# Two-layer transformer step on one core: weight rounding, probability scaling and the differential heads' small operations change engine or shape

## The chip, the cores and the metric

The kernel runs on one core of one Trainium2 chip, in one launch. The metric is device microseconds. Three runs of the kernel before took 935.11, 935.13 and 935.72 us, a median of 935.13 us.

## The reference

256 tokens of width 1024 (one batch) go through two transformer blocks, all in fp32. What matters here is the second block: 16 meta tokens are put in front (272 keys), one input projection feeds two attentions, and a gated sum of the two goes through an output projection and a gated MLP.

The first of the second block's attentions is banded: 16 query heads on 4 key heads, head width 64, a window of 128 positions, all meta keys, and a sink logit that has no value; its softmax therefore runs over 272 scores and the sink. The second is differential: 8 heads with two query/key pairs each,

```python
p = jax.nn.softmax(s, axis=-1)
a = p[:, :, 0] - lam * p[:, :, 1]
o = rms_norm(einsum(a, v), subln_gain) * (1.0 - lambda_init)
```

dense over the 272 keys. The first block has a smaller banded attention (8 query heads on 2 key heads, 256 keys and a sink) beside a retention layer.

## The kernel before

**Split products.** fp32 accuracy comes from three products per matrix: the weight and the activation are each written as a rounded high part and the low remainder, and high*high, high*low and low*high are added in PSUM (`PASS`). So each weight must be split on chip. Weights come as 272 units of 128x1024 (`wstream`). `fetch` (L283 to L302) does one unit: SP issues the load into `raw` (4 buffers); `hi` is `raw` rounded; `lo` is `raw - hi`, on DVE in two pieces of 512 columns (L301). The rounding has two forms. Where `hi_pool` is false, ACT does it in two pieces of 512 columns (L299). Where it is true, GpSimd (POOL) does all 1024 columns in one instruction (L296). `next_unit` splits one unit ahead of the one that is asked for. `hi_pool` is true for two units at the very start and, set after the V projections of the second block, for the 38 units that are split during its two attentions; it is set false again when the branch projections begin.

**Second block's attentions.** `keys` and `proj_a` project two feature tiles (48 matmuls of 128x128 by 256 or 272 columns); `rope_T` copies the result out on ACT (L501, L503), swaps halves with four small DMAs that ACT issues (L505, L506), and multiplies and adds on DVE (L507) and POOL (L508, L511). `stack_q` and `stack_k` split the result again: `qe`, `qo`, `ks` are rounded on ACT, their low parts come from POOL (L521, L522, L537) and DVE (L536). The scores follow on TensorE (L544, L545, mask L547).

**Banded attention** (`sink_attention`, `sink_softmax`): per query head a row minimum on DVE (`mn`, L552), the exponential on ACT with its row sum (`p`, L562), a reciprocal on DVE (`rc`, L564), and the scaling of the 272 (first block: 128 or 256) probabilities to `pn` on ACT (L565). Then four heads are transposed on TensorE (L580), split into `pt` on ACT and DVE (L327, L328), and multiplied with V (`o_ps`, L584). There are 32 such heads and query tiles in the second block, 16 in the first.

**Differential heads** (L929 to L989): for each of 8 heads and each of 2 query tiles, two scores, two `mn`, two exponentials into `p` (L942, 6 buffers) with their sums in two 1-wide tiles `den0`, `den1`; then on DVE, per query tile, `e2` (L946), `rc` (L949), `rl` (L951), all one element per row, and `a` = `p0` + `rl` * `p1` (L954). After both query tiles `a` is transposed (L960, L965), copied by ACT (L962, L967), multiplied with V (`od_ps`, L972 to L974), normalized and transposed again.

**Order.** The tile framework sets each engine's instruction order when the program is built: a planner runs the whole program through its own model of costs and gives each engine a fixed list. The engines then run these lists in order, with semaphores between them. So matmuls of later projections stand between those of the attention, where the planner expected room. PSUM banks and SBUF tiles are shared by tag as `BANKS`, `ROT` and `BUFS` say.

Of the kernel before, what the change touches and what calls it, by code (L numbers as in the profile page):

```python
# [12 lines left out]
AF = mybir.ActivationFunctionType  # L13
ALU = mybir.AluOpType
# [7 lines left out]
NKEY = NTOK + NMETA  # L22
EPS = 1e-6
# [4 lines left out]
# products of parts (weight, x), 0 high, 1 low; what needs the low part of x goes last where x comes late  # L28
PASS = ((0, 0), (0, 1), (1, 0))
PARTS = (((0, 0), (1, 0)), ((0, 1),))  # L30
WB = 5  # units of split weights on chip
AHEAD = 1  # units split before they are asked for
LAG = 4  # last units of an output projection, done token tile by token tile
# [4 lines left out]
VB1 = 2  # the second half of V of the differential heads follows this head group of the window attention  # L38
PIECE = 512  # columns of a unit split at a time
# PSUM banks by tag, and which of them each kind of use takes in turn, part by part of the program  # L40
# [8 lines left out]
# tiles per name in each phase  # L49
# [10 lines left out]
# ---------------------------------------------------------------- host layout  # L60
# [162 lines left out]
# ---------------------------------------------------------------- the kernel  # L223
class Body:
# [22 lines left out]
    # ---- small helpers  # L247
    def banks(self, name):
        """how the spare PSUM bank "x" is shared out from here on"""
        self.rot = {k: [0, v.split()] for k, v in ROT[name].items()}  # L250
# [25 lines left out]
    def t(self, shape, name, dt=F32, tag=None):  # L276
        """a tile of the current phase"""
        tag = tag or name
        return self.rp.tile(shape, dt, tag=tag, bufs=self.bufs.get(tag, 1), name=name)
# [24 lines left out]
    def spare(self, skip, tags):  # L304
        """big tiles that nothing else needs for now hold units, from the skip-th that is still to be fetched"""
        u = self.un + skip
        for tag in tags:
            if tag == "DE":
                self.place[u] = [self.bp.tile([P, UC], F32R, tag="D", name=f"hi{u}"),
                                 self.bp.tile([P, UC], F32R, tag="E", name=f"lo{u}")]  # L310
                u += 1
            else:
                t = self.bp.tile([P, 2, 2, UC], F32R, tag=tag, name=f"w{u}")
                for i in range(2):
                    self.place[u] = [t[:, i, 0], t[:, i, 1]]
                    u += 1
# [84 lines left out]
    def sumsq(self, h, np_=P):  # L401
        """sum of squares of h [np_, 1024] (or of two psum halves) per partition, in two halves"""
        nc = self.nc
        xn = self.t([P, D], "xn")
        ss = self.sm(2, "ss")
        for c in range(2):
            s = slice(512 * c, 512 * c + 512)
            src = h[c] if isinstance(h, list) else h[:np_, s]
            nc.scalar.activation(out=xn[:np_, s], in_=src, func=AF.Square, accum_out=ss[:np_, c:c + 1])
        return xn, ss  # L410
# [16 lines left out]
    def to_T(self, xn, c, dst, t0, np_=P):  # L427
        """four feature tiles of xn (half c) transposed, split into dst"""
        nc = self.nc
        b = self.tp([P, 4, np_], "xt_ps")  # L430
        for j in range(4):
            k = 4 * c + j
            nc.tensor.transpose(b[:, j, :], xn[:np_, k * P:(k + 1) * P], self.ident[:np_, :np_])
        self.split(dst[:, 0, 4 * c:4 * c + 4, t0:t0 + np_], dst[:, 1, 4 * c:4 * c + 4, t0:t0 + np_], b)
# [11 lines left out]
    def mm_a(self, out, unit, XT, n0, n1, kn=8, j=0):  # L446
        """out[128, n1-n0] = W^T X^T for the j-th 128 columns of the unit"""
        nc = self.nc
        wv = [w.rearrange("p (k c) -> p k c", k=kn) for w in unit]
        i = 0  # L450
        last = 3 * kn - 1
        for k in range(kn):
            for a, b in PASS:
                nc.tensor.matmul(out, wv[a][:, k, j * P:(j + 1) * P], XT[:, b, k, n0:n1],  # L454
                                 start=(i == 0), stop=(i == last))
                i += 1

    def mm_b(self, out, unit, XT, t0, t1, kn, k0, c0, cn, start, stop):
        """out[tokens, cn] += X[tokens, k-tiles] W"""
        nc = self.nc  # L460
        wv = [w.rearrange("p (k c) -> p k c", k=kn) for w in unit]
        i = 0
        last = 3 * kn - 1
        for k in range(kn):
            for a, b in PASS:
                nc.tensor.matmul(out, XT[:, b, k0 + k, t0:t1], wv[a][:, k, c0:c0 + cn],  # L466
                                 start=(start and i == 0), stop=(stop and i == last))
                i += 1

    def mm_group(self, out, us, XT, t0, t1, kn, cn):  # L470
        """out[tokens, cn] = X[tokens] W over all units; the low parts of X come last, they are ready last"""
        nc = self.nc
        ws = [[w.rearrange("p (k c) -> p k c", k=kn) for w in u] for u in us]
        seq = [(j, k, a, b) for part in PARTS for j in range(len(us)) for k in range(kn) for a, b in part]
        for i, (j, k, a, b) in enumerate(seq):
            nc.tensor.matmul(out, XT[:, b, kn * j + k, t0:t1], ws[j][a][:, k, :cn],  # L476
                             start=(i == 0), stop=(i == len(seq) - 1))

    def group_b(self, XT, toks, kn, nh, cn, name):
        """X @ W for one group of columns over nh units; one psum bank per token range"""  # L480
# [6 lines left out]
    def rope_T(self, ps, m, n, tab, half, out=None, scale=1.0):  # L487
        """ps [128, m, n] feature-major, times scale; returns fp32 SBUF tile"""
        nc = self.nc
# [19 lines left out]
        if out is None:  # L509
            out = t1  # L510
# [3 lines left out]
    def stack_q(self, qf):  # L514
        """qf [128, 2, 256] -> QE, QO [128, 2, 256]: hi and lo stacked on the contraction rows"""
        nc = self.nc
# [8 lines left out]
    def stack_k(self, kf, n):  # L525
        """kf [128, n] (two heads) -> [(KS, KL)] * 2"""
# [14 lines left out]
    def scores(self, out, q, k, k0, k1, mask=None):  # L541
        """out[128, k1-k0] = q^T k (all four partial products), mask = (index, first column)"""
# [12 lines left out]
    def sink_softmax(self, s, n, nsink, out):  # L555
        """s [128, n + 1] in PSUM, negated scores, the last column for the sink; out [128, n] = softmax(-s)"""
# [8 lines left out]
        nc.scalar.activation(out=out, in_=p[:, :n], func=AF.Copy, scale=rc)  # L565

    def sink_attention(self, q, kst, vs, sink, ktiles, masks, OT, c, qt):
        """one kv head and one query tile: four q heads"""
# [43 lines left out]
    def out_proj(self):  # L612
        """psum banks [t][c] of a product X @ W of 1024 columns"""
# [11 lines left out]
    def out_last(self, acc, jobs, t, major=False):  # L625
        """the last units for token tile t, one bank after the other"""
# [6 lines left out]
    # ---- block 1  # L633
    def block1(self):
# [22 lines left out]
        # v of the retention, token-major  # L657
# [53 lines left out]
        # sliding window attention  # L711
# [20 lines left out]
        # gates and branches  # L732
# [38 lines left out]
        for t in range(2):  # L771
# [8 lines left out]
            # relu(r z)^2 = r^2 relu(z)^2: the row factor of the norm goes on after the second product  # L780
# [44 lines left out]
    # ---- block 2  # L825
    def block2(self):
# [6 lines left out]
        for t in range(2):  # L833
            self.out_last(acc, jobs, t)
            # both norms in one: with m = mean(h^2) + eps and hf = h * g_fin, x2 = hf / sqrt(m) and its own mean
            # square plus eps is (mean(hf^2) + eps * m) / m
# [44 lines left out]
        def v_T(m, name):  # L881
            """V^T of m feature tiles, transposed: per token range a psum bank [tokens, m * 128]"""
# [19 lines left out]
        self.hi_pool = True  # L902
# [24 lines left out]
        for pr in range(4):  # L927
            kb = keys()
            q = self.stack_q(self.rope_T(self.proj_a(XT, name="q_ps"), 2, NTOK, rope_b, 32, scale=-0.125))  # L929
            for m in range(2):  # L930
                h = 2 * pr + m
                am = []
                e2 = self.sm(2, "e2")
                for qt in range(2):
                    ps, den = [], []
                    for e in range(2):
# [4 lines left out]
                        d = self.sm(1, f"den{e}")  # L941
                        nc.scalar.activation(out=p[:, :NKEY], in_=s, func=AF.Exp, bias=nm, scale=-1.0, accum_out=d)  # L942
                        ps.append(p)
                        den.append(d)
                    # den0 * (softmax 0 - lam softmax 1): the norm that follows takes den0 out, its eps times den0^2
                    nc.vector.scalar_tensor_tensor(out=e2[:, qt:qt + 1], in0=den[0], scalar=EPS, in1=den[0],  # L946
                                                   op0=ALU.mult, op1=ALU.mult)
                    rc = self.sm(1, "rc")
                    nc.vector.reciprocal(rc, den[1])  # L949
                    rl = self.sm(1, "rl")  # L950
                    nc.vector.scalar_tensor_tensor(out=rl, in0=rc, scalar=self.nlam, in1=den[0],  # L951
                                                   op0=ALU.mult, op1=ALU.mult)
                    a = self.t([P, NKEY + 2], "a")
                    nc.vector.scalar_tensor_tensor(out=a[:, :NKEY], in0=ps[1][:, :NKEY], scalar=rl,  # L954
                                                   in1=ps[0][:, :NKEY], op0=ALU.mult, op1=ALU.add)
# [65 lines left out]
        def post(t, acc, gain):  # L1021
            """x[t] += rmsnorm(acc[t]) * gain, by halves"""
# [73 lines left out]
# ---------------------------------------------------------------- launch  # L1096
# [34 lines left out]
```

## Time and profile before

| | |
|---|---|
| median of three runs | 935.13 us |
| span of the profiled execution, first to last instruction | 927.7 us |
| TensorE (PE) busy | 895.6 us, 97% |
| DVE busy | 632.9 us, 68% |
| ACT busy | 495.1 us, 53% |
| POOL busy | 221.8 us, 24% |
| granted TensorE clock, mean | 0.994 |

The profile gives the span of the profiled execution, and no device time of its own beside it; the median lies 7.4 us above the span. Busy shares are means over stages. The second block's attentions run from about 433 to 632 us of the span. PE's busy time is that of pipelined matmuls whose ends are modelled: a matmul of 256 columns is shown with some 285 ns, while 48 of them take 5.74 us, one each 120 ns. A hole of less than about 160 ns between two matmuls is therefore not seen as idle time.

### The profile page before, as it was taken

The numbers are of one execution on the slowest core, as the hardware profiler recorded it, in microseconds if no ns is written. First come the engines' busy times: TensorE is split into PE (matmuls) and PEld (weight loads), VectorE is DVE, ScalarE is ACT, GpSimd is POOL, SyncE is SP. The second block draws the span as 40 slices with busy tenths as digits, with TensorE's granted clock in tenths as the row PEclk, the third lists the DMA queues.
The fourth block names the chain that finished last, engine by engine and source line by source line (L and its number), as shares of the span: only waits on it lengthen the run. The fifth ranks groups of instructions, "written<-read, shape, count | busy, mean of one in ns | idle before, by whom it ended". The sixth has DMA issues, their size and how long they took to land.

```text
span 927.7 us, 16499 instructions
## 1 busy us (share of the span) xinstructions
PE 895.6 (97%) x6188; PEld 819.8 (88%) x6188; DVE 632.9 (68%) x1177; ACT 495.1 (53%) x1100; POOL 221.8 (24%) x219
## 2 busy tenths in 40 slices
PE   6999899999999999999979999999999999999997
PEld 4899889998889999978978888798999799999996
DVE  5556887577755455565889999997567665655554
ACT  4544368555554554554237786576455454444442
POOL 3012550011000000012795757652011100000000
PEclk9999999999999999999999999999999999999999
DMA  8675554468666656663744344343466666665551
GB/s 287 242 212 154 160 154 137 137 204 290 206 189 183 185 185 191 189 203 111 211 135 144 99 126 123 105 135 104 135 186 211 232 197 195 187 190 186 183 160 45
DMA packets 48128, 160.20 MB, mean 173 GB/s; under 512 B 6432, under 2 KB 8224, under 8 KB 48048
## 3 DMA queue, kind: packets, MB, share of 16 engines
q1 hardware_dynamic: 43376, 153.95, 52.7%
q10 hardware_dynamic: 4672, 5.20, 2.0%
q8 instruction: 48, 0.79, 0.4%
q14 instruction: 32, 0.26, 0.1%
HBM read 151.83 MB, written 2.10 MB: 166 GB/s over the span
## 4 chain that ended last, share of the span: by engine, by line
PE 77%; DVE 8%; DMA 5%; POOL 4%; issue 3%; ACT 2%; ACTq 0%; SPq 0%; POOLq 0%; DVEq 0%
PE op L466 21%; PE fi_ps L454 12%; PE f_ps L454 9%; PE gate_ps L454 7%; DVE lo L301 5%; PE ru_ps L454 3%; PE gr_ps L454 2%; PE bd_ps L454 2%; PE vr_ps L476 2%; PE bs_ps L454 2%; DMA sw<-t 2%; DMA raw<-in_wstream_dram 2%; PE vb_ps L476 2%; PE fi_ps L476 1%; PE au_ps L454 1%
## 5 line engine op out<-in xcount | busy, mean ns | idle before, releaser
L301 DVE TENSOR_TENSOR lo<-raw,hi 128x512 fp32r<-128x512 f32 x536 | 385.9, 762 | 196.7 <-ACT hi L299 188.3
L299 ACT CAST hi<-raw 128x512 fp32r<-128x512 f32 x456 | 258.8, 618 | 240.0 <-issue 84.4
L466 PE MATMUL op<-hi,hid 128*128 128x512 f32 x416 | 131.3, 396 | 0.0
L454 PE MATMUL fi_ps<-xf2t,hi 128*128 128x256 f32 x640 | 115.8, 283 | 0.0
L454 PEld LDWEIGHTS fi_ps<-xf2t,hi 128*128 128x128 f32 x640 | 100.3, 191 | 1.0
L466 PEld LDWEIGHTS op<-hi,hid 128*128 128x128 f32 x416 | 76.3, 188 | 16.7
L454 PE MATMUL fi_ps<-xf2t,lo 128*128 128x256 f32 x320 | 90.5, 283 | 0.0
L466 PE MATMUL op<-lo,hid 128*128 128x512 f32 x208 | 81.4, 393 | 0.0
L454 PE MATMUL f_ps<-xf1t,hi 128*128 128x256 f32 x448 | 81.4, 283 | 0.0
L454 PEld LDWEIGHTS f_ps<-xf1t,hi 128*128 128x128 f32 x448 | 70.7, 191 | 1.3
L454 PE MATMUL f_ps<-xf1t,lo 128*128 128x256 f32 x224 | 63.3, 282 | 0.0
L454 PEld LDWEIGHTS fi_ps<-xf2t,lo 128*128 128x128 f32 x320 | 61.2, 191 | 0.0
L296 POOL TENSOR_SCALAR hi<-raw 128x1024 fp32r<-128x1024 f32 x40 | 48.8, 1223 | 35.8 <-PE k_ps L454 13.5
L415 POOL TENSOR_SCALAR e<-ss 128x1 f32<-128x1 f32 (+1 forms) x11 | 3.3, 303 | 223.8 <-ACT py L1027 195.0
L795 POOL TENSOR_TENSOR sq<-relu 128x512 f32<-128x512 f32 x14 | 15.8, 1129 | 152.4 <-ACT relu L792 152.4
L454 PE MATMUL q_ps<-x2t,hi 128*128 128x256 f32 x256 | 49.6, 287 | 0.0
L454 PE MATMUL gate_ps<-x1t,hi 128*128 128x256 f32 x256 | 49.4, 287 | 0.0
L454 PE MATMUL gate_ps<-x2t,hi 128*128 128x256 f32 x256 | 48.7, 284 | 0.0
L466 PEld LDWEIGHTS op<-lo,hid 128*128 128x128 f32 x208 | 39.0, 188 | 9.2
L454 PEld LDWEIGHTS f_ps<-xf1t,lo 128*128 128x128 f32 x224 | 42.8, 191 | 0.1
L454 PEld LDWEIGHTS gate_ps<-x2t,hi 128*128 128x128 f32 x256 | 40.0, 189 | 1.1 <-issue 1.0
L454 PEld LDWEIGHTS q_ps<-x2t,hi 128*128 128x128 f32 x256 | 40.2, 189 | 0.7 <-issue 0.5
(297 smaller groups left out, 2090.3 us busy)
## 6 DMA issues: line engine op xcount, KB each, us to landing
raw<-in_wstream_dram SPq DMA_DIRECT2D x272, 512.0 KB, 3.7
sw<-t ACTq DMA_DIRECT2D x40, 64.0 KB, 3.4
x<-in_x_dram SPq DMA_DIRECT2D x3, 512.0 KB, 6.8
sw<-t ACTq DMA_DIRECT2D x40, 34.0 KB, 2.5
sw<-t ACTq DMA_DIRECT2D x8, 128.0 KB, 4.7
g_pre<-in_gains_dram SPq DMA_DIRECT2D x2, 512.0 KB, 6.2
x<-hf SPq DMA_DIRECT2D x2, 512.0 KB, 2.7
x<-x SPq DMA_DIRECT2D x2, 512.0 KB, 5.8
```

The costliest lines, as they stand in the source:

```text
L296: nc.gpsimd.tensor_scalar(out=hi, in0=raw, scalar1=1.0, scalar2=0.0, op0=ALU.mult, op1=ALU.add)
L299: nc.scalar.copy(hi[:, c:c + PIECE], raw[:, c:c + PIECE])
L301: nc.vector.tensor_sub(lo[:, c:c + PIECE], raw[:, c:c + PIECE], hi[:, c:c + PIECE].bitcast(F32))
L415: nc.gpsimd.tensor_scalar(out=e[:np_], in0=ss[:np_, 0:1], scalar1=1.0 / D, scalar2=EPS, op0=ALU.mult, op1=ALU.add)
L454: nc.tensor.matmul(out, wv[a][:, k, j * P:(j + 1) * P], XT[:, b, k, n0:n1], start=(i == 0), stop=(i == last))
L466: nc.tensor.matmul(out, XT[:, b, k0 + k, t0:t1], wv[a][:, k, c0:c0 + cn], start=(start and i == 0), stop=(stop and i == last))
L476: nc.tensor.matmul(out, XT[:, b, kn * j + k, t0:t1], ws[j][a][:, k, :cn], start=(i == 0), stop=(i == len(seq) - 1))
L795: nc.gpsimd.tensor_tensor(out=q, in0=r, in1=r, op=ALU.mult)
```

## The change

Three edits; comments were removed as well, which changes no instruction.

- `hi_pool` is no longer set true ahead of the second block's attentions, so their 38 units are rounded on ACT in two pieces (L299) in place of POOL in one (L296).
- The scaling of the banded probabilities (`pn`) goes from an ACT activation to a DVE `tensor_scalar`, in both blocks, since both use `sink_softmax`.
- In the differential heads all four exponentials of a head come first, their sums in two 2-wide tiles; `rc`, `rl` and `e2` are done once for both query tiles, two elements per row; then the two `a`.

```diff
@@ sink_softmax
-        nc.scalar.activation(out=out, in_=p[:, :n], func=AF.Copy, scale=rc)
+        nc.vector.tensor_scalar(out=out, in0=p[:, :n], scalar1=rc, scalar2=None, op0=ALU.mult)
@@ block2
         kts = [(0, P), (P, P), (NTOK, NMETA)]
-        self.hi_pool = True
@@ block2, differential heads
-                am = []
-                e2 = self.sm(2, "e2")
+                den = [self.sm(2, f"den{e}") for e in range(2)]
+                ps = []
                 for qt in range(2):
-                    ps, den = [], []
                     for e in range(2):
                         ...
-                        d = self.sm(1, f"den{e}")
-                        nc.scalar.activation(out=p[:, :NKEY], in_=s, func=AF.Exp, bias=nm, scale=-1.0, accum_out=d)
+                        nc.scalar.activation(out=p[:, :NKEY], in_=s, func=AF.Exp, bias=nm, scale=-1.0,
+                                             accum_out=den[e][:, qt:qt + 1])
                         ps.append(p)
-                        den.append(d)
-                    nc.vector.scalar_tensor_tensor(out=e2[:, qt:qt + 1], in0=den[0], scalar=EPS, in1=den[0],
-                                                   op0=ALU.mult, op1=ALU.mult)
-                    rc = self.sm(1, "rc")
-                    nc.vector.reciprocal(rc, den[1])
-                    rl = self.sm(1, "rl")
-                    nc.vector.scalar_tensor_tensor(out=rl, in0=rc, scalar=self.nlam, in1=den[0],
-                                                   op0=ALU.mult, op1=ALU.mult)
+                rc = self.sm(2, "rc")
+                nc.vector.reciprocal(rc, den[1])
+                rl = self.sm(2, "rl")
+                nc.vector.scalar_tensor_tensor(out=rl, in0=rc, scalar=self.nlam, in1=den[0],
+                                               op0=ALU.mult, op1=ALU.mult)
+                e2 = self.sm(2, "e2")
+                nc.vector.scalar_tensor_tensor(out=e2, in0=den[0], scalar=EPS, in1=den[0],
+                                               op0=ALU.mult, op1=ALU.mult)
+                am = []
+                for qt in range(2):
                     a = self.t([P, NKEY + 2], "a")
-                    nc.vector.scalar_tensor_tensor(out=a[:, :NKEY], in0=ps[1][:, :NKEY], scalar=rl,
-                                                   in1=ps[0][:, :NKEY], op0=ALU.mult, op1=ALU.add)
+                    nc.vector.scalar_tensor_tensor(out=a[:, :NKEY], in0=ps[2 * qt + 1][:, :NKEY],
+                                                   scalar=rl[:, qt:qt + 1], in1=ps[2 * qt][:, :NKEY],
+                                                   op0=ALU.mult, op1=ALU.add)
                     am.append(a)
```

## Rows read from the trace of the kernel before

**Rows 1.** Windows: us, then busy us (instructions) by engine, PEclk, DMA share, GB/s.

```profile
460.00:490.00 30.00, 24.95 (x187) 23.70 (x186) 24.95 (x39) 11.08 (x29) 27.81 (x20) 0.94 0.47 139
490.00:540.00 50.00, 47.74 (x349) 41.79 (x348) 47.56 (x113) 37.57 (x99) 32.00 (x27) 1.00 0.44 126
...
632.00:660.00 28.00, 27.95 (x214) 25.95 (x215) 20.58 (x58) 16.55 (x55) 2.14 (x4) 1.00 0.39 113
460.00:620.00 160.00, 148.77 (x1098) 134.23 (x1097) 146.87 (x306) 101.71 (x275) 110.69 (x93) 0.99 0.42 123
```

**Rows 2.** Waits of PE over the span: total us, times, longest us.

```profile
PE s L544 <- POOL qe L521: 4.2, 1, 4.2
PE o_ps L584 <- DVE pt L328: 3.7, 2, 2.0
...
PE s L544 <- ACT p L562: 2.1, 1, 2.1
```

**Rows 3.** Timeline of POOL, 455 to 486 us: start us, us, engine, line.

```profile
465.33 1.49 POOL L296 TENSOR_SCALAR hi<-raw 128x1024 fp32r<-128x1024 f32 x1
...
468.47 1.71 POOL L508 TENSOR_TENSOR sw<-sw,rope_b 128x512 f32<-128x512 f32 x1
470.15 1.48 POOL L296 TENSOR_SCALAR hi<-raw 128x1024 fp32r<-128x1024 f32 x1
471.72 1.76 POOL L521 TENSOR_TENSOR qe<-t,qe 64x512 fp32r<-64x512 f32 x1
```

**Rows 4.** Timeline of ACT, same stretch; idle time before and its releaser in brackets.

```profile
460.55 0.60 ACTq L506 DMA_DIRECT2D sw<-t  x1
...
468.54 0.62 ACT L519 CAST qe<-t 64x512 fp32r<-64x512 f32 x1 [4.17 <-POOL t L511]
```

**Rows 5.** Timeline of PE, same stretch.

```profile
473.53 0.59 PE L544 MATMUL s<-ks,qe 128*128 128x272 f32 x1 [4.25 <-POOL qe L521]
```

**Rows 6.** Groups by form, 430 to 660 us: busy us, mean ns | idle before.

```profile
L301 DVE TENSOR_TENSOR lo<-raw,hi 128x512 fp32r<-128x512 f32 x100 | 88.7, 927 | 9.7 <-POOL hi L296 5.0 <-ACT hi L299 4.6
...
L296 POOL TENSOR_SCALAR hi<-raw 128x1024 fp32r<-128x1024 f32 x38 | 46.7, 1232 | 34.9 <-PE k_ps L454 13.5 <-PE vb_ps L476 11.8 <-PE gate_ps L454 3.2
...
L565 ACT ACTIVATE pn<-p,rc 128x272 f32<-128x272 f32 x32 | 15.9, 520 | 6.2 <-DVE rc L564 5.1 <-DVE of L590 0.9
...
L299 ACT CAST hi<-raw 128x512 fp32r<-128x512 f32 x25 | 14.1, 616 | 4.4 <-PE vb_ps L476 3.5 <-PE s L545 0.6 <-PE bs_ps L454 0.2
...
L954 DVE SCALAR_TENSOR_TENSOR a<-p,rl 128x272 f32<-128x272 f32 x16 | 12.4, 782 | 0.5
...
L951 DVE SCALAR_TENSOR_TENSOR rl<-rc,nlam,den 128x1 f32<-128x1 f32 x16 | 6.9, 430 | 0.4
...
L946 DVE SCALAR_TENSOR_TENSOR e<-den 128x1 f32<-128x1 f32 x16 | 3.9, 247 | 0.6 <-ACT p L942 0.6
...
L949 DVE RECIPROCAL rc<-den 128x1 f32<-128x1 f32 x16 | 2.5, 155 | 2.0 <-ACT p L942 1.8
```

**Rows 7.** Line L301, 230 to 420 us: duration ns min/median/max.

```profile
L301 DVE TENSOR_TENSOR lo<-raw,hi x130: 678/684/694, 229.4 to 411.7; 128x512 fp32r<-128x512 f32 x130
```

**Rows 8.** Line L954, whole span: duration ns min/median/max.

```profile
L954 DVE SCALAR_TENSOR_TENSOR a<-p,rl x16: 481/500/1598, 558.3 to 649.8; 128x272 f32<-128x272 f32 x16
```

**Rows 9.** Line L699, whole span.

```profile
L699 DVE TENSOR_SCALAR ry<-ro,mv,rq x8: 537/544/547, 77.3 to 130.7; 128x256 f32<-128x256 f32 x8
```

**Rows 10.** Timeline of POOL, 522 to 536 us.

```profile
527.47 1.50 POOL L296 TENSOR_SCALAR hi<-raw 128x1024 fp32r<-128x1024 f32 x1
```

**Rows 11.** Timeline of DVE, same stretch.

```profile
527.98 1.26 DVE L328 TENSOR_TENSOR os_t<-of,os_t 128x256 fp32r<-128x256 f32 x1
529.16 1.76 DVE L301 TENSOR_TENSOR lo<-raw,hi 128x512 fp32r<-128x512 f32 x1
```

**Rows 12.** Timeline of ACT, same stretch.

```profile
531.51 0.49 ACT L562 ACTIVATE p<-s,mn 128x273 f32<-128x273 f32 x1 [3.27 <-DVE mn L552]
```

**Rows 13.** Windows, first block's attention, columns as in rows 1.

```profile
100.00:160.00 60.00, 56.06 (x444) 54.15 (x443) 47.28 (x113) 40.52 (x103) 20.79 (x20) 0.97 0.49 151
```

## Prediction

> **What bounds the kernel now.** Read first the granted clock and the busy shares by stretch. PE is at 97% of the span, but not evenly. In the 28 us from 632, where the attentions run out, PE issues 214 matmuls, 7.64 per us, with no idle time worth the name; in the 160 us from 460 to 620 it issues 1098, 6.86 per us, and the view calls it busy for 148.8 us [rows 1]. The mix of shapes is much the same in both, so an estimate of what PE itself needs there is 1098 / 7.64 = 143.7 us: up to 16.3 us of the stretch is lost. Outside the second block's attentions PE is dense, and what a stage before or after them gains is not at issue. In that stretch DVE is busy 146.9 us of 160 and in the 50 us from 490 even 47.6, 95%; POOL 110.7; ACT 101.7, 64% [rows 1]. So PE is fed by two engines that are full, DVE throughout and POOL from 460 to 490 (27.8 of 30).
>
> Then the waits of PE, which name who ends its holes. The three longest kinds inside the stretch are the scores behind POOL's `qe` (4.2 us, once), V products behind DVE's `pt` (3.7), and scores behind the exponential `p` (2.1): 10.0 us together [rows 2]. The rest of the 16.3 are holes shorter than a matmul's shown duration.
>
> The timelines say why. Before `qe` POOL works off a list with no hole: between 465.33 and 473.5 two weight roundings of 1.49 and 1.48 us stand in front of it [rows 3]; ACT sits idle 4.17 us for a POOL result [rows 4] and PE 4.25 us for `qe` [rows 5]. The clock falls in that stretch alone: 0.94 as mean of 460 to 490, against 1.00 from 490 to 540, though waits of some 2 us lie there too [rows 1, 2]. 0.06 of 30 us is 1.8 us, the price of the long hole beyond itself.
>
> DVE is full partly because it is held. `lo` takes 684 ns where POOL is quiet [rows 7] and 927 ns on average over 100 of them here [rows 6]: 100 x 0.243 = 24.3 us. `rl`, one element per row, takes 430 ns where the reciprocal of the same size takes 155: 16 x 0.275 = 4.4. `a` takes 782 on average and 500 as median, 16 x 0.28 = 4.5 [rows 6, 8]. One case in full: POOL's rounding runs from 527.47 for 1.50 us, `os_t` starts on DVE inside it and takes 1.26, the next `lo` 1.76 [rows 10, 11], and the exponential behind them leaves ACT idle for 3.27 us [rows 12]. All three kinds together lose 33 us, and the roundings are about 30 x 1.232 = 37 of POOL's 110.7 us, a third [rows 1, 6] (30 of their 38 lie between 460 and 620). So about 11 us of DVE's time are due to them.
>
> **The change part by part.** The sums are made against the profiled execution, span 927.7 us; the median of 935.13 lies 7.4 above it, and I carry a saving over one to one.
>
> Rounding on ACT. POOL loses 38 x 1.232 = 46.7 us. ACT gains 76 x 0.616 = 46.8 us; the row of the same operation in the same stretch has 616 ns [rows 6]. What goes:
> (a) the chain in front of `qe`: 1.49 + 1.48 = 2.97 us of the 4.2 [rows 2, 3]. The remaining 1.2 is shorter than the waits that left the clock at 1.00, so the dip's 1.8 goes too: -4.8. Covered by ACT's own 4.17 us of idle time there [rows 4], which holds three pairs of roundings; without that cover ACT's `qe` rounding comes one pair, 1.2 us, later.
> (b) a third of the 5.8 us of waits that DVE ends (3.7 directly, 2.1 through `p`) [rows 2]: -1.9.
> (c) short holes: 16.3 - 10.0 = 6.3 us, of which I take a third again: -2.1. What is late next is DVE still, and POOL's `qe`, `t` and `kl`, which go on holding it.
>
> What it costs: ACT goes from 101.7 us to 101.7 + 37.0 - 15.9 = 122.8 of 160, 77%; beside that it issues four DMAs of some 0.60 us for each rotation [rows 4], behind whatever rounding is queued ahead of them, and its list holds exponentials, `pt`, `at` and `ks`, whose successors are DVE, POOL and PE. Each rounding pair placed ahead of one that PE awaits costs 1.23 us. Below: none, since ACT idles 37 us net of the load. Above: a third of the 30 pairs, 12.3. I take two pairs, +2.5, nearer the low end, because the planner does know ACT's load. SP's queue keeps its loads; a `raw` buffer comes free when `lo` has read it, as before, and the 0.42 DMA share leaves room [rows 1].
>
> Scaling on DVE. ACT loses 32 x 0.520 = 15.9 us [rows 6] (and 16 smaller ones in the first block). DVE gains 32 operations that the trace does not show. Below: 0.155 us, a one-element operation [rows 6], 5.0 in all. Above: `a`, the same width with two inputs, held by POOL as it is now, 0.782, 25.0 in all. Nearest is a `tensor_scalar` of 256 elements with two scalars, out of PSUM, 0.544 [rows 9]; I take it: +17.4 us of DVE time.
>
> The small operations. Eight each of `rl`, `e2` and `rc` go: 8 x (0.430 + 0.247 + 0.155) = 6.7 us of DVE [rows 6]; that two elements cost as much as one is the assumption, and its error is of the size of an element. Against it the first `a` now waits for the second query tile's exponentials, so one more `a` (0.5 us [rows 8]) stands behind the last of them: 8 x 0.5 = 4.0 us if nothing covered it, 0 if projections do. I take 0, since PE has projections to run in between.
>
> DVE altogether: -11 - 6.7 + 17.4 = -0.3 us. So DVE is not relieved by the sum, only the places of its holds change; that is why (b) and (c) are no more than a third. With the two bounds of the scaling it is -12.7 and +7.3, and (b) and (c) become about 7 and 1.
>
> Here a rule bears on the sum. Every row with two SBUF inputs above is lengthened while POOL runs; the rule in the Trainium skill, page "SBUF — State Buffer", section "Who interferes with whom", is that DVE and POOL share one port pair as an exclusive lock, and it counts `tensor_scalar` from SBUF to SBUF among the operations that take it. So the moved scaling can itself be held by POOL, and hold it, which ACT's could not. The page "VectorE: DVE Perf Modes", section "The perf-mode tier table (the rule you actually need)", gives such an fp32 operation two elements per cycle; an estimate from its figures is (150 + 136) / 0.96 = 298 ns for 272 elements. By that alone, 9.5 us instead of 17.4, the time would be 1 to 2 us shorter; with the lock's holds added it is near the row again.
>
> First block: ACT 40.5 of 60 us, DVE 47.3, POOL 20.8 [rows 13]; sixteen scalings change engine there. DVE gains at most 16 x 0.54 = 8.7 us in 60, to 93%. PE is 94% busy. I take 0, bounds -1 and +2.
>
> Sum: -4.8 - 1.9 - 2.1 + 2.5 = -6.3, so 935.1 - 6.3 = 929 us.
>
> One thing no row shows: the lists of all engines are planned anew, with other costs, so instructions move against each other everywhere from the first block's attention on. I give this 2 us either way.
>
> **The rivals.**
> A. POOL was the root of nearly all: with a third of its work gone, DVE's holds shrink by more than the roundings' share (a POOL operation that is not queued behind a rounding also collides less), and the scaling is at the low bound. Then most of the 16.3 us come back and the dip with them. For it: POOL has no hole in front of `qe` [rows 3]. Against: two thirds of POOL's work stay. -13 or so: 922 us.
> B. The holes only change their owner: ACT at 77% and its DMA issues end what POOL and DVE ended; (a) holds, and two to four more pairs wait in front of PE. 935 us.
> C. Slower: ACT's list becomes the bound of the differential heads. There a rounding pair lies in front of `p`, `at` or `od_t`; all scores, copies and squares go through ACT, and every rotation's DMAs as well. The gains are 8.8 us, so it decides from 8.8 / 1.23, some 7 of 30 pairs, on. With a third, 10, and the exposed `a` tails of 8 x 0.5 less what projections cover, half: -8.8 + 12.3 + 2 = +5.5, 940.6 us. For it: ACT has 23% left and six kinds of work in one list. Against: ACT's long idle stretches now are waits for POOL and DVE [rows 4, 12], just what becomes shorter.
>
> **How the numbers follow.** Forecast 0.45 (929, own range 924 to 933), A 0.20, B 0.13, C 0.22. The range of 920 to 941 holds the forecast, B, and most of A and of C. A difference under 0.2%, 1.9 us, can't be told from none. Faster: the forecast, A, and a little of B, less the forecast's upper end: 0.65. Same: 0.13. Slower: 0.22.
>
> **What would show it.** Right: no wait of PE for `qe` over 2 us and a clock of 1.00 from 460 to 490; mean `lo` under 850 ns in the attentions; POOL at some 74 of 160 us; ACT near 123; PE over 7.1 matmuls per us. For the scaling: its mean against 0.544. Wrong: PE's waits ended by ACT's `p`, `at` or `qe` adding to over 10 us, `lo` waiting on ACT's `hi`, or a mean of `lo` that does not fall.

## The result, and the profile after

924.7 us, median of four runs (921.33 to 926.7), against 935.12 us before: a ratio of 0.9882 with a 95% interval of 0.9858 to 0.9906. That is 10.4 us faster, where 6.3 were forecast (929; range 920 to 941). The profiled executions, 927.7 us of span before and 924.9 after, lie only 2.8 us apart; the section on the repeated kernels comes back to this. Two executions stand outside all ratios, one of the kernel before at 1751.25 us and one of the write-only run, its profiled one, at 984.21 us with a granted clock of 0.85.

The windows of the changed kernel answer to [rows 1]: us, busy us (instructions) of PE, weight loads, DVE, ACT, POOL, then granted clock, DMA share, GB/s.

```profile
460.00:490.00 30.00, 26.29 (x206) 24.82 (x205) 26.75 (x43) 18.57 (x42) 19.08 (x14) 1.00 0.63 187
490.00:540.00 50.00, 47.90 (x351) 42.24 (x351) 49.14 (x127) 39.29 (x99) 23.06 (x18) 1.00 0.38 114
...
460.00:620.00 160.00, 152.41 (x1132) 137.32 (x1131) 149.07 (x326) 123.00 (x310) 78.61 (x67) 1.00 0.45 133
```

PE issues 1132 matmuls in the stretch where it issued 1098. ACT is at 123.0 us, POOL at 78.6, and DVE, at 149.1, is no emptier than before. The clock is whole in every stretch shown.

The waits of PE from 430 to 660 us, for [rows 2]:

```profile
PE o_ps L584 <- DVE of L590: 1.6, 2, 1.3
PE s L544 <- ACT p L562: 1.5, 2, 0.8
PE vb_ps L454 <- ACT vt L888: 1.4, 1, 1.4
PE k_ps L454 <- ACT ms L600: 1.1, 1, 1.1
PE o_ps L584 <- DVE pt L328: 0.6, 2, 0.4
```

The wait for `qe` of 4.2 us is gone, the one for `pt` fell from 3.7 to 0.6. New ones end on ACT: `vt` and the gate's `ms`. On ACT's timeline `ms` stands behind a pair of roundings; in front of `vt` ACT itself sat idle for 1.22 us. On POOL's, ACT's and PE's timelines the place of [rows 3, 4, 5] reads so; first POOL:

```profile
469.74 1.63 POOL L511 TENSOR_TENSOR t<-t,sw 128x512 f32<-128x512 f32 x1
472.19 1.46 POOL L508 TENSOR_TENSOR sw<-sw,rope_b 128x512 f32<-128x512 f32 x1 [0.82 <-DMA sw<-t]
473.73 1.61 POOL L511 TENSOR_TENSOR t<-t,sw 128x512 f32<-128x512 f32 x1
475.42 1.62 POOL L521 TENSOR_TENSOR qe<-t,qe 64x512 fp32r<-64x512 f32 x1
```

then ACT:

```profile
468.76 2.17 ACT L299 CAST hi<-raw 128x512 fp32r<-128x512 f32 x4
471.40 0.62 ACT L519 CAST qe<-t 64x512 fp32r<-64x512 f32 x1 [0.47 <-POOL t L511]
```

and PE at its first scores:

```profile
477.20 0.29 PE L544 MATMUL s<-ks,qe 128*128 128x272 f32 x1
```

ACT does roundings in time that it used to spend idle: 0.47 us of idle time are left in front of `qe`, in place of 4.17. On POOL the roundings are gone, but `qe` is no earlier. The `t` that ACT's `qe` waits for ends at 471.37; then POOL waits 0.82 us for a DMA of the next rotation and does that rotation's `sw` and `t` before `qe`, which ends at 477.04, against 473.48 in [rows 3]. PE waits for it no more because it has other work: 70 matmuls of the V projection (`vb_ps`) stand between the projection of q and the first scores, where 48 stood before. DVE's groups from 430 to 660 us answer to [rows 6]:

```profile
L301 DVE TENSOR_TENSOR lo<-raw,hi 128x512 fp32r<-128x512 f32 x104 | 86.4, 865 | 13.9 <-ACT hi L299 13.8
L565 DVE TENSOR_SCALAR pn<-p,rc 128x272 f32<-128x272 f32 x32 | 13.9, 462 | 0.2
...
L954 DVE SCALAR_TENSOR_TENSOR a<-p,rl 128x272 f32<-128x272 f32 x16 | 9.9, 653 | 0.0
...
L946 DVE SCALAR_TENSOR_TENSOR rl<-rc,nlam,den 128x2 f32<-128x2 f32 x8 | 2.3, 289 | 0.1
...
L944 DVE RECIPROCAL rc<-den 128x2 f32<-128x2 f32 x8 | 1.3, 160 | 1.5 <-ACT p L939 1.3
L949 DVE SCALAR_TENSOR_TENSOR e<-den 128x2 f32<-128x2 f32 x8 | 1.2, 148 | 0.0
```

`lo` takes 865 ns where it took 927, `a` 653 where it took 782. The small operations cost 2.3 + 1.3 + 1.2 = 4.8 us in place of 6.9 + 2.5 + 3.9 = 13.3, and the scaling 13.9.

Laid over POOL's timeline, `lo` shows what a mean hides. From 430 to 680 us of the kernel before, 56 pieces of `lo` ran beside no operation of POOL, with a mean of 682 ns, and 58 beside one, with 1124. In the changed kernel 71 ran beside none (683) and 45 beside one (1129). A piece that meets POOL is held as long as before; fewer of them meet it.

### The profile page after: what moved, and what is told of

It is laid out like the page before. It is cut to its first block, busy times and chain, and to the rows that moved or that the text cites. A ratio compares the mean times of both kernels' runs of the same rounds, so it can differ in the third digit from the quotient of the medians.

```text
span 924.9 us, 16482 instructions
## 1 busy us (share of the span) xinstructions
PE 896.0 (97%) x6188; PEld 819.9 (89%) x6188; DVE 627.7 (68%) x1201; ACT 516.5 (56%) x1128; POOL 174.7 (19%) x181
## 5 line engine op out<-in xcount | busy, mean ns | idle before, releaser
L301 DVE TENSOR_TENSOR lo<-raw,hi 128x512 fp32r<-128x512 f32 x536 | 380.5, 751 | 195.1 <-ACT hi L299 190.5
L299 ACT CAST hi<-raw 128x512 fp32r<-128x512 f32 x532 | 301.9, 618 | 244.3 <-issue 84.7
L795 POOL TENSOR_TENSOR sq<-relu 128x512 f32<-128x512 f32 x14 | 15.8, 1132 | 152.0 <-ACT relu L792 152.0
L454 PEld LDWEIGHTS gate_ps<-x1t,hi 128*128 128x128 f32 x256 | 40.3, 191 | 0.2
```

Source lines behind the costliest of these rows:

```text
L299: nc.scalar.copy(hi[:, c:c + PIECE], raw[:, c:c + PIECE])
L301: nc.vector.tensor_sub(lo[:, c:c + PIECE], raw[:, c:c + PIECE], hi[:, c:c + PIECE].bitcast(F32))
L795: nc.gpsimd.tensor_tensor(out=q, in0=r, in1=r, op=ALU.mult)
```

## The experiments

Each was timed against the kernel before on the same chip: the first four on one chip, the others on another, where the changed kernel itself was not timed. The median of the kernel before is 934.6 us on the first and 934.83 to 935.47 on the other. My theory at the start: the rounding off POOL is the gain, the other two parts are near nothing. Its rivals: DVE's shorter list is the gain, or the rounding pays only with ACT relieved.

**The two kernels again.**

> The kernel before, unchanged. Two readings of the times: in the profile of before the span is 927.7 us and the median time 935.1, 7.4 us apart; in the profile of after the same run has 924.9 and 926.7, 1.8 apart. If what lies around the span is 1.8 us for both kernels, the profiled execution of before was some 5.6 us quicker than the timed ones, and this run shows a span of some 933 us beside a time of 935. If the kernel before really has more around its span, it shows some 928 beside 935.

Measured: 935.05 us (0.9994, 0.9967 to 1.0021), and the profiled execution took 935.5 with a span of 933.5 us. So 2 us lie around the span, not 7.4, and the execution that the prediction read, 927.7 us of span, was a quick one: the runs of the kernel before on this chip go from 930.78 us (mean granted clock 0.994) to 940.56 (0.986). Where the difference lies, in this profile of the same instructions:

```profile
460.00:490.00 30.00, 24.37 (x177) 23.25 (x176) 24.96 (x36) 11.11 (x30) 28.99 (x20) 0.89 0.48 144
490.00:540.00 50.00, 47.86 (x331) 41.37 (x330) 47.62 (x111) 38.29 (x102) 32.48 (x27) 0.95 0.41 122
540.00:580.00 40.00, 38.31 (x280) 34.38 (x280) 36.56 (x80) 26.90 (x71) 21.97 (x20) 0.98 0.35 104
580.00:632.00 52.00, 50.52 (x370) 46.04 (x369) 47.93 (x96) 31.58 (x92) 33.24 (x31) 0.97 0.39 124
```

Its waits of PE:

```profile
PE s L544 <- POOL qe L521: 5.4, 1, 5.4
PE o_ps L584 <- DVE pt L328: 3.2, 2, 1.7
PE s L544 <- ACT p L562: 2.0, 1, 2.0
PE at_ps L960 <- DVE a L954: 1.3, 1, 1.3
```

The same holes, and behind three of them the clock at its lower level for a while: 30 x 0.11 + 50 x 0.05 + 40 x 0.02 + 52 x 0.03 = 8.2 us at most, against 1.8 in the first profile. One of the three is the wait for `p`: 2.13 us, at 530 us of the first profile, left the clock at 1.00; 2.02 us, at the same place of the repeat, were followed by 0.50.

> The changed kernel, unchanged, on the chip of the runs beside it: 921 to 927 us, ratio 0.986 to 0.991, if its spread of 5 us belongs to the executions; a narrower group near one end if it belongs to the chips.

Measured: 925.59 us (0.9893, 0.9856 to 0.993), 922.92 to 927.58; the spread belongs to the executions. Its first window, columns as above:

```profile
460.00:490.00 30.00, 27.56 (x218) 26.14 (x217) 26.68 (x50) 18.66 (x43) 17.89 (x13) 1.00 0.66 198
```

The clock is whole here in every window from 433 to 660 us. Set against the profile of the kernel before on the same chip: up to 8.2 us of clock, and the four waits of PE shown above, 5.4 + 3.2 + 2.0 + 1.3 = 11.9 us, of which the changed kernel keeps a part.

How much of the gain is clock, all executions tell better than two profiles. All nine of the changed kernel had a mean clock of 0.994 to 0.998 and took 921.33 to 927.58 us, median 925.2. Ten of the kernel before, on the two chips, had 0.994 to 0.997 as well; they took 930.78 to 934.6, median 932.4. So some 7 of the 10 us are there at a like clock, and the clock is about 3.

**The three parts, alone and in pairs.** The edit of each run is the part's own piece of the change; the others stay as before.

> Only the rounding moves to ACT; the scaling stays on ACT and the small operations as they were. My theory (POOL freed in front of qe and DVE held less): most of the gain, 926 to 929 us. The rival (the rounding only pays because the scaling left ACT): ACT has 101.7 + 37.0 = 139 of 160 us of work, its list is late, and the time is 933 to 940.

> Scaling on DVE and small operations at once, with the rounding left on POOL. My theory: near the kernel before, 933 to 938 us, since DVE gains some 7 to 10 us of work, held by POOL, and loses 7. The rival (the gain is DVE's shorter list and the shorter chain per head): 925 to 930.

> Rounding on ACT and the small operations at once, scaling left on ACT. Rounding alone gave 0.9908. If the scaling on DVE is a cost that the rounding pays for (it was part of the pair that gave 1.0091), this is as quick as the full change or quicker: 920 to 926 us. If the scaling is needed to relieve ACT, it is slower than the full change: 927 to 932.

> Rounding on ACT and scaling on DVE, small operations as before. If joining the small operations is worth DVE's 6.7 us of them, 926 to 930 us; if it is hidden, the time of the full change, 923 to 927.

> Only the scaling moves to DVE. My theory after the pair's 1.0091: the scaling is the cost, held by POOL's roundings on the shared side: 940 to 946 us. The rival (the joined tail of the heads is the cost): 933 to 937.

> Only the small operations of the differential heads at once. If the later first a of each head is exposed, 936 to 940 us; if DVE's 6.7 us of work less count, 929 to 933; as predicted, with neither, 933 to 936.

```
rounding  scaling  small ops   median us   ratio    95% interval
ACT       ACT      apart       927.29      0.9908   0.9878 to 0.9938
ACT       ACT      joined      926.37      0.9916   0.9888 to 0.9943
ACT       DVE      apart       923.53      0.9886   0.9847 to 0.9925
ACT       DVE      joined      925.59      0.9893   0.9856 to 0.9930
POOL      DVE      apart       945.96      1.0126   1.0093 to 1.0158
POOL      DVE      joined      943.24      1.0091   1.0063 to 1.0119
POOL      ACT      joined      934.19      0.9987   0.9964 to 1.0010
```

The rounding alone is nearly all of the gain. The small operations are nothing beyond the measurement, with or without the rest. The scaling has no price of its own: with the rounding on POOL it costs 1.3%, with the rounding on ACT it costs nothing (whether it gains the last 0.2% these intervals don't tell). Rounding with joined small operations, 926.37 us, fell between its two forecasts and decides neither. My theory's forecast for the pair without the rounding, 933 to 938, was too low, and the rival that the rounding needs ACT relieved (933 to 940) fell: rounding alone has ACT at 131.6 us of 160, and PE is busy for all of the 50 us from 490 to 540. Its windows, columns as above:

```profile
460.00:490.00 30.00, 27.09 (x191) 25.62 (x191) 25.64 (x39) 18.41 (x44) 16.83 (x12) 0.89 0.63 194
490.00:540.00 50.00, 50.00 (x383) 45.58 (x382) 44.67 (x105) 45.91 (x117) 23.08 (x20) 1.00 0.43 125
...
460.00:620.00 160.00, 157.09 (x1172) 144.34 (x1172) 138.90 (x299) 131.59 (x329) 71.63 (x63) 0.98 0.48 142
```

and behind the attentions

```profile
660.00:690.00 30.00, 27.02 (x203) 25.92 (x204) 16.62 (x27) 14.07 (x31) 4.28 (x4) 0.94 0.35 109
```

It has no wait for `qe` either, and yet the clock falls from 460 to 490, behind a wait of 2.2 us for `p`. Its other loss is at the end of the last head.

Why the scaling turns is in its own durations. Source rows of `pn`, min/median/max ns, in the changed kernel from 470 us on:

```profile
L565 DVE TENSOR_SCALAR pn<-p,rc x32: 329/354/1499, 486.3 to 558.7; 128x272 f32<-128x272 f32 x32
```

and with the scaling alone on DVE, the rounding still on POOL:

```profile
L565 DVE TENSOR_SCALAR pn<-p,rc x32: 346/924/1448, 484.1 to 577.0; 128x272 f32<-128x272 f32 x32
```

354 ns against 924 as median; its group there is 26.3 us (mean 851) against 13.9. Laid over POOL's timeline: with the rounding on POOL, 10 of the 32 ran beside no operation of POOL and took 346 to 363 ns, 22 beside one, with a median of 1135; in the changed kernel 22 ran beside none (329 to 363) and 10 beside one (median 498). One place of that kernel, POOL's timeline and then DVE's:

```profile
518.68 1.49 POOL L296 TENSOR_SCALAR hi<-raw 128x1024 fp32r<-128x1024 f32 x1
520.25 1.27 POOL L522 TENSOR_TENSOR qo<-t,qo 64x512 fp32r<-64x512 f32 x1
521.60 0.75 POOL L537 TENSOR_TENSOR kl<-t,ks 64x272 fp32r<-64x272 f32 x1
```

```profile
519.38 3.12 DVE L565 TENSOR_SCALAR pn<-p,rc 128x272 f32<-128x272 f32 x3
```

Three scalings, which end within 0.2 us of the ends of POOL's three operations, take 3.12 us, where three of the median of 354 ns take 1.06. What PE then waits for in that kernel:

```profile
PE o_ps L584 <- DVE pt L328: 8.3, 3, 4.2
PE s L544 <- POOL qe L521: 6.3, 1, 6.3
PE s L544 <- ACT p L562: 3.1, 3, 2.6
PE pt_ps L580 <- DVE pn L565: 2.4, 3, 1.0
```

while DVE is full and ACT at half:

```profile
460.00:620.00 160.00, 139.07 (x972) 125.04 (x971) 154.48 (x301) 77.58 (x206) 105.97 (x86) 0.94 0.38 115
```

**POOL's work given back, with no use.** The full change, and per unit on POOL a one-column read of `raw` and two operations on a scratch tile `sc`, which nothing reads:

```diff
+        if self.extra:   # the 38 units of the attentions
+            nc.gpsimd.tensor_scalar(out=sc[:, 0:1], in0=raw[:, 0:1], scalar1=1.0, scalar2=0.0, op0=ALU.mult, op1=ALU.add)
+            for c in range(0, UC, PIECE):
+                nc.gpsimd.tensor_scalar(out=sc, in0=sc, scalar1=1.0, scalar2=0.0, op0=ALU.mult, op1=ALU.add)  # or: nc.gpsimd.memset(sc, 0.0)
```

> The full change, with work on POOL that nobody needs in the place where the roundings were: for each of the 38 units a one-column read of raw and two operations of 128x512 that read and write a scratch tile in SBUF, beside the computation, which is unchanged. If POOL's roundings cost by holding DVE and by standing in POOL's list, this gives their cost back: 936 to 946 us, pn at 0.7 to 0.9 us. If the gain came from where hi is made (two pieces, sooner after the load), the time stays at 923 to 927.

> The same, but the two operations only write the scratch tile (memset). The POOL list is as long if a memset takes as long as a copy. If what costs is standing in POOL's list in front of qe and the rotations, the time is that of the reading one. If what costs is the holding of DVE operations with two SBUF inputs by POOL's reads, lo stays near 0.86 and only pn, if anything, is held: 925 to 931 us.

Measured: with reads 944.61 us (1.0111, 1.0079 to 1.0144), 19 us above the changed kernel's 925.59 on the other chip; with writes alone 938.53 (1.0035, 1.0013 to 1.0057), 13 us above. The reading one brings the pair's loss back with the computation of the full change, so POOL's occupation is enough to cost that much. It is more of it than the roundings were, 73.8 us against 46.7, so the run does not show that where `hi` is made is worth nothing. POOL also waits 32.1 us in front of its reads of `raw`, mostly for loads, as it waited 34.9 in front of the roundings [rows 6]. It also answers a rival that the edit carries with it, that the new order of instructions is the gain: at the first scores, here 72 matmuls of the V projection stand ahead, near the changed kernel's 70, and the gain is gone. With reads, the two longest of PE's waits are

```profile
PE o_ps L592 <- DVE pt L334: 7.1, 6, 1.9
PE vb_ps L462 <- ACT vt L896: 4.3, 1, 4.3
```

and none is for `qe`: it is not POOL's list in front of `qe` that PE's waits name here, but DVE first. Groups from 430 to 680 us with reads, DVE then POOL:

```profile
L302 DVE TENSOR_TENSOR lo<-raw,hi 128x512 fp32r<-128x512 f32 x108 | 94.6, 909 | 16.2 <-ACT hi L300 16.0
L573 DVE TENSOR_SCALAR pn<-p,rc 128x272 f32<-128x272 f32 x32 | 19.2, 615 | 0.1
```

```profile
L307 POOL TENSOR_SCALAR sc<-sc 128x512 f32<-128x512 f32 x72 | 55.7, 774 | 4.4
L305 POOL TENSOR_SCALAR sc<-raw 128x1 f32<-128x1 f32 x36 | 18.1, 503 | 32.1 <-DMA raw<-in_wstream_dram 30.5
```

and with writes alone (of this profile only the durations of DVE and POOL are read):

```profile
L302 DVE TENSOR_TENSOR lo<-raw,hi 128x512 fp32r<-128x512 f32 x102 | 85.8, 879 | 15.4 <-ACT hi L300 15.2
L573 DVE TENSOR_SCALAR pn<-p,rc 128x272 f32<-128x272 f32 x32 | 18.9, 612 | 0.2
```

```profile
L307 POOL MEMSET sc<- 128x512 f32 x76 | 40.6, 534 | 3.2
L305 POOL TENSOR_SCALAR sc<-raw 128x1 f32<-128x1 f32 x38 | 11.7, 308 | 55.6 <-DMA raw<-in_wstream_dram 53.5 <-ACT t L511 0.9
```

The mean of `pn` is the same with writes as with reads (612 and 615 ns, against 462 without), below the 700 to 900 that I expected with reads. The means mix in POOL's other operations, so the timelines are laid over each other again. `pn` beside memsets alone, 5 of them, took 344 to 691 ns, and beside no operation of POOL, 8, 336 to 361. `lo` beside memsets alone, 9 pieces, took 674 to 693 ns, as beside none; beside `tensor_scalar` operations alone in the reading run, 28 pieces, up to 1102 with a mean of 789. My forecast of 925 to 931 for the writes was wrong, as was the one of "the same as with reads". How much of the 13 us is the longer POOL list and how much the held scaling these two runs do not split, as a memset (534 ns) is shorter than a copy (774) and the reading kernel's POOL work longer, 73.8 us against 52.3.

**Two tries for more.**

```diff
-        nc.vector.tensor_scalar(out=out, in0=p[:, :n], scalar1=rc, scalar2=None, op0=ALU.mult)
+        if self.flip: (as above)  else: nc.scalar.activation(out=out, in_=p[:, :n], func=AF.Copy, scale=rc)
+        self.flip = not self.flip
```

> The full change, with every second banded scaling back on ACT. With the rounding on ACT the scaling is nearly free on either engine (rounding alone 0.9908, with the scaling 0.9886): shares between the two engines, 922 to 926 us. If DVE (149 of 160 us) sets the pace of what is left, 919 to 923.

Measured: 930.1 us (0.9946, 0.9924 to 0.9967), outside both forecasts and slower than the scaling wholly on either engine. In its windows the loss lies in two places, at the first scores and, where the changed kernel has none, at the last differential head's end:

```profile
460.00:490.00 30.00, 25.68 (x183) 24.55 (x183) 26.60 (x42) 17.15 (x40) 17.30 (x12) 0.90 0.60 191
...
660.00:690.00 30.00, 27.93 (x205) 26.73 (x204) 15.40 (x24) 12.56 (x29) 3.90 (x3) 0.89 0.39 123
```

2.1 us of holes and 30 x 0.11 = 3.3 us of clock in the second alone. The last head ended there after the projections that would have covered it; the rounding-only run loses time at the same place. I put it down to the order that was planned, which differs with the engine of the 24 scalings; no run shows that.

```diff
-AHEAD = 1
+AHEAD = 2
```

> The full change, with units split two ahead of the one asked for instead of one. If what is left is that weights come late behind other work of ACT and DVE, holes go: 917 to 923 us. If not, 924 to 930, since splits taken earlier stand in front of softmax work.

Measured: 928.78 us (0.993, 0.9905 to 0.9956), in the second range: splitting weights sooner does not help. Neither beats the changed kernel, nor does any of the parts clearly.

## Why the prediction was right, and where its sizes were not

The direction and the stage were right, and so was the cause in the main: POOL's roundings cost, and DVE is held by what runs on POOL. Several sizes agree by luck, and term (a) came true by another mechanism than the one that it names. ACT's load came out as worked out (123.0 us; 122.8 forecast), `qe` holds PE no more, and the clock is whole from 460 to 490. PE issues 7.08 matmuls per us in the profiled run and 1159 / 160 = 7.24 in the second one, above 7.1 as asked in one of two. `lo` at 865 ns missed the 850: two thirds of POOL's work stayed, and went on holding it. Of the 11 us of DVE's time that the prediction put down to the roundings, `lo` and `a` gave back 5.5 + 2.1 = 7.6. Its hold of `rl` was read too high: the 8 that ran beside no operation of POOL took 202 to 221 ns, not the reciprocal's 155, so 16 x 0.215 = 3.4 us were lost there and not 4.4.

*Term (a), the clock's 1.8 us.* This term was mis-sized, and its reason does not hold. It came from one execution, in which the clock fell only behind the longest hole. In the repeat of the kernel before it fell three times, 8.2 us at most, and in the changed kernel's repeat not at all from 433 to 660 us; over all executions the clock is worth about 3. The prediction took it that waits of some 2 us leave the clock at 1.00; the wait for `p` was followed by 0.50 in the repeat and in the rounding-only run. The prediction carried its saving over to a median that lies 7.4 us above the span. That gap was a sign that the profiled execution was quicker than the timed ones: in the repeat and after, time less span is 1.8 to 2. From that quick execution to the two profiles of the changed kernel the gain is 2.8 and 6.6 us, so that the sum of 6.3 lies near the measured 10.4 is in part luck.

*Term (a), POOL's list, 3.0 us.* The whole wait went (4.2, and 5.4 in the repeat), but not by a chain that is 3.0 us shorter. From the first matmul of the q projection to the first scores it is 27.6 and 28.8 us in the two profiles of the kernel before, and 28.4 and 26.9 in the two of the changed one; in the reading run, with POOL's work back, it is 34.7. PE waits no more because the planned order puts 22 more matmuls of the V projection in between; at 0.13 us each, the rate of the 48 before, they are 2.9 us. The prediction had the new order only as 2 us either way. Whether that order would close the hole with the rounding on POOL, no run tests.

*Term (b), 1.9 us of DVE's 5.8.* `pt` and `p` fell together from 5.8 to 2.1, 3.7 us, twice the forecast; but `of` took 1.6 of it back. Why more than a third went is not shown.

*Term (c)* can't be seen by itself. *ACT's price, +2.5:* new waits on `vt`, `ms` and `t` sum to 1.4 + 1.1 + 0.4 = 2.9, in the repeat to 0.5 + 0.6 = 1.1. Of these `ms` stands behind a pair of roundings, while before `vt` ACT was idle. So the size is near, and only a part of it is the price that the prediction meant.

*The scaling, +17.4 us of DVE.* The single number hid two: 26.3 with the rounding on POOL and 13.9 without, and a change of 1.3% or none in the time. The prediction summed parts that do not add: it priced the scaling by a row out of PSUM (544 ns), which POOL does not hold (three of those eight ran beside a POOL operation and took 544 to 547 ns), and its sum has that one price, though it says that POOL can hold the scaling. The total for DVE was near (149.1 us against 146.9 before, -0.3 forecast), with terms that were off both ways. By itself this part costs 10.5 us, more than rival C's 5.5 and by another cause. The first block's sixteen scalings, put at 0, can't be told from 0: the second block's V projection begins at 417.5 and 416.4 us in the changed kernel's profiles and at 416.2 in the rounding-only run, which leaves them on ACT.

What the Trainium skill says in "SBUF — State Buffer", section "Who interferes with whom", that `tensor_scalar` can take the port pair that DVE shares with POOL and that the one that issues second then waits for the whole instruction of the other, agrees with this case's trace: 1135 ns as median beside an operation of POOL, 355 beside none, and ends that follow POOL's. The estimate of 298 ns, from the Trainium skill's "VectorE: DVE Perf Modes" in the prediction, is somewhat low; the quickest of 32 took 329.

*The small operations.* 8.5 us off DVE (6.7 forecast), and no time, as forecast; the later first `a` did not show either. DVE's time there was not what PE waited for.

*The rivals.* A (922) asked for the scaling at the low bound and the holes nearly gone; the time lies between it and the forecast, and about 3 us of the 10 were the clock. B and C did not come: ACT at 131.6 us of 160, with the scaling still on it, holds PE less than POOL did.

*The plan, 2 us either way.* Perhaps too little: the half-and-half scaling and the second unit ahead moved the time by 3 to 5 us, but they change more than the order, and no run changes the order alone.

## What to carry to other kernels

Before moving work to the engine that a profile shows as full, look at which of its operations take longer than their own minimum, and beside what: here taking the roundings off POOL alone gave 0.9%, taking 8.5 us off DVE's own list gave nothing that shows, and the same scaling was dear or free by where the roundings ran. When a wait is gone, look whether its chain became shorter or PE got other work in between. Where edits touch the same shared resource, measure them in pairs; their prices do not add. And when span and median of a profile differ by more than a few us, read the times and clocks of other executions before pricing a hole.

## What the runs showed of the hardware

A hole of PE can cost more than itself: in the profile of the kernel before, behind the wait of 4.2 us, the granted clock is 0.50 from 474 to 476 us and PE issues 11 matmuls in these 2 us, against 18 in the 2 us from 478, at 1.00. It does not do so each time: behind the same wait for `p` of 2.1 and 2.0 us the clock stayed at 1.00 in one execution and went to 0.50 in another. Over executions of one and the same kernel the mean clock went from 0.997 to 0.986; in the changed kernel it was 0.994 to 0.998.

DVE's `tensor_scalar` in SBUF is lengthened beside POOL's `memset`, which only writes (344 to 691 ns, against 336 to 361 beside none). `lo`, a `tensor_tensor` with two SBUF inputs, is not (674 to 693 against 669 to 694); beside POOL operations that read, it is (668 to 1102 in the reading run).
